# One PSUM tile per bank, with halved evacuations and another order at the start of each FFN and of the convolution

## The chip, the core and the metric

The kernel runs on one core of one Trainium2 chip. TensorE (PE) multiplies, VectorE (DVE) and ScalarE (ACT) do the elementwise work, GpSimd (POOL) does little here, and SyncE (SP) issues the weight loads. The metric is the time of one execution in device microseconds (us); the median of a few runs is compared. PSUM, into which TensorE writes, has eight banks of 128 partitions by 512 float32.

## What is computed

An encoder of four layers on 256 tokens of width 1024. Each layer is a half-step SwiGLU FFN, one token mixer, and a second half-step FFN; the four mixers are dilated attention, a convolution module, a Fourier mixer and a chunked gated linear attention (GLA). Each sub-layer starts with an RMS norm, and a last one ends the trunk.

```python
def _swiglu(h, w1, w3, w2):
    return (jax.nn.silu(h @ w1) * (h @ w3)) @ w2          # 1024 -> 2816 -> 1024

def reference(x, norm_g, ...):
    h = x
    for i in range(DEPTH):                                # 4 layers, mixer m = i % 4
        h = h + 0.5 * _swiglu(_rmsnorm(h, norm_g[i, 0]), ffn_w1[i, 0], ffn_w3[i, 0], ffn_w2[i, 0])
        u = _rmsnorm(h, norm_g[i, 1])
        ...                                               # mix = attention, convolution, Fourier or GLA of u
        h = h + mix
        h = h + 0.5 * _swiglu(_rmsnorm(h, norm_g[i, 2]), ffn_w1[i, 1], ffn_w3[i, 1], ffn_w2[i, 1])
    return _rmsnorm(h, final_norm_g)

def _conv_module(u, w_pw1, b_pw1, w_dw, b_dw, ln_g, ln_b, w_pw2, b_pw2):
    a, gate = jnp.split(u @ w_pw1 + b_pw1, 2, axis=-1)
    z = a * jax.nn.sigmoid(gate)
    ...                                                   # depthwise convolution of width 31, LayerNorm, silu, w_pw2
```

## The kernel before

**Numbers.** Every float32 operand of a matmul is a pair: a rounded high part and the rest as a low part, and a product is three matmuls (high by high, high by low, low by high). In the FFN, `wide` packs two of the three into one matmul of 512 columns, so that a result stands in two halves q=0 and q=1 of a bank, which are added when it is read.

**Weights.** All weights come as blocks of 128 by 2048 float32 (1 MB), in one fixed order. SP loads a block into one of four `raw` buffers (L158); `split_block` makes the pair `w` (four buffers): ACT copies the high part (L167), and DVE subtracts it from `raw` for the low part (L170). After the matmuls of a block `done()` counts a free buffer in `pend`; `pump(n)` issues up to n of the splits that are pending at that place in the code, with `between` ahead of the DVE half. The instructions of each engine run in the order in which the code issues them, and the framework sets semaphores between engines from the tiles that instructions read and write.

**PSUM.** The eight banks are four tiles `P00` to `P11` of [128, 1024], each two banks; `bank(half, j)` is a half of such a tile and `two(half, n)` a whole one. In the rows both are called P. `ab()` gives out the four banks of one half in turn, `dbank(j)` those of the other.

**FFN** (`ffn`). The 2816 hidden columns go in NG = 11 groups of 256: each takes a block of w1 into PA and one of w3 into PB, 32 matmuls per block (16 of 256 columns and 16 of 512), and every second group is followed by a block of w2 (`half_add`) into the other four banks. What follows a group is: `parts`, an ACT copy of q=1 out of PSUM (L461); `add`, the DVE addition of q=0 (L465); `times_r`, the norm's factor (L468); silu (L471); `gate` (L474) and the split of its result `g` (L622 on ACT, L623 on DVE). `half_close` adds the finished banks to the residual h (L277). The factor R of the norm comes from `stats` and three Newton `steps` on DVE.

**Mixers.** Projections go into `ab()` banks and are evacuated singly: in attention `qk` (L1017), the scores' `s` (L1046) and `og`; in the convolution `ar` (L694) and `gr` (L699) of the gated linear unit, then `zp` (L704); in the Fourier mixer `m` (L623); in GLA `ks` (L1237, L1244) and per head and chunk `t` (L1391). Each mixer ends with a down projection that is added to h (L277, L280).

**What sets the order.** There is no planner. TensorE's program order is the code's; between it and the two elementwise engines only the semaphores decide.

Of the kernel before, what the change touches and what calls it, by code (L numbers as in the profile page):

```python
# [18 lines left out]
NG = DFF // 256  # L19
# [19 lines left out]
class Enc:  # L39
    def __init__(self, ctx, tc, a, stages):  # L40
        self.ctx, self.tc, self.nc, self.a = ctx, tc, tc.nc, a
        self.stages = stages
        P = lambda name, bufs=1, **kw: ctx.enter_context(tc.tile_pool(name=name, bufs=bufs, **kw))
        self.const = P("const")
        self.wp = P("wp")
        self.hp = P("hp")
        self.ev = None
        self.ps = P("ps", space=PSUM)
        self.dram = P("dram", space=bass.MemoryType.DRAM)
        self.nm = 0  # L50
        self.banks = [[self.ps.tile([128, 1024], F32, name=f"P{i}{n}") for n in range(2)] for i in range(2)]
        self.lower, self.nab, self.held = 0, 3, []


# [16 lines left out]
        return self.bank(1 - self.lower, j)  # L71

    def bank(self, half, j):
        return self.banks[half][j // 2][:, 512 * (j % 2):512 * (j % 2) + 512]

    def two(self, half, n):

        return self.banks[half][n].rearrange("p (c q n) -> p c q n", c=2, q=2)

    def mm(self, out, lhsT, rhs, start, stop):  # L80
        return self.nc.tensor.matmul(out, lhsT, rhs, start=start, stop=stop, skip_group_check=True)  # L81
# [177 lines left out]
    def close_pair(self, j, P, scale, bias=None):  # L259

        nc = self.nc
        h = self.h[j]
        P = P if isinstance(P, list) else [self.v2(P)]
        if self.unperm:
            assert bias is None
            hn = self.sb(self.ev, [128, 2, 256], F32, "sl", 2)
            for p in P[1:]:
                nc.vector.scalar_tensor_tensor(h, p, float(scale), h, ALU.mult, ALU.add)
            for c in range(2):
                nc.vector.scalar_tensor_tensor(hn[:, c].rearrange("p (m a) -> p a m", a=4),  # L270
                                               P[0][:, c].rearrange("p (a m) -> p a m", a=4), float(scale),
                                               h[:, c].rearrange("p (a m) -> p a m", a=4), ALU.mult, ALU.add)
            nc.gpsimd.tensor_copy(h, hn)
            h = hn
        elif bias is None:
            for p in P:
                nc.vector.scalar_tensor_tensor(h, p, float(scale), h, ALU.mult, ALU.add)  # L277
        else:
            for c in range(2):
                nc.vector.scalar_tensor_tensor(h[:, c], P[0][:, c], bias[c], h[:, c], ALU.add, ALU.add)  # L280
        self.flush_acc()
        if j < 3 or not (self.short() or self.row_norm()):
            self.normed(j, h)
            self.square(j, h)
        else:
            self.square(j, h)
            self.normed(j, h)
# [145 lines left out]
    def wide(self, p, c, w, k, x, start, stop):  # L433


        self.mm(p[:, c, 0], w[:, 1, k], x[:, 0], start, False)
        self.mm(p[:, c], w[:, 0, k], x, False, stop)

    def ffn(self, l, s):
        nc = self.nc  # L440
# [6 lines left out]
        PA, PB = (self.two(up_half, n) for n in range(2))  # L447
# [6 lines left out]
        def take_up(n, i, P):  # L454
            up(self.take((n, i)), P)
            self.done()

        def parts(P, tag):

            t = self.sb(self.ev, [128, 2, 256], F32, tag, 2)  # L460
            nc.scalar.activation(t, P[:, :, 1], AF.Copy)  # L461
            return t

        def add(t, P):
            nc.vector.tensor_tensor(t, t, P[:, :, 0], ALU.add)  # L465

        def times_r(t):
            nc.vector.tensor_tensor(t, t, self.Rb(), ALU.mult)  # L468

        def silu(t):  # L470
            nc.scalar.activation(t, t, AF.Silu)  # L471

        def gate(i, sl, br):
            nc.vector.tensor_tensor(br, sl, br, ALU.mult)  # L474
            g[i] = self.pair(self.ev, [128, 2, 256], "g", NG)
            self.split(br, g[i])
# [5 lines left out]
        for n, ks in enumerate(cuts):  # L482
# [20 lines left out]
        br0 = parts(PB, "br")  # L503
        steps.pop(0)()
        add(br0, PB)
        self.pump(held)
        steps.pop(0)()
        for i in range(1, NG):
            take_up("w1", i, PA)
            sl = parts(PA, "sl")  # L510
            if i == 1:
                add(sl, PA)
                times_r(sl0)
                silu(sl0)
                self.pump(1, between=lambda: times_r(sl))
                silu(sl)
                times_r(sl0)
                gate(0, sl0, br0)
                self.pump(1)
            else:  # L520
                self.pump(1, between=lambda: (add(sl, PA), times_r(sl)))
                silu(sl)
            if i == 4 and pre:
                self.pre = pre()
            take_up("w3", i, PB)
            br = parts(PB, "br")
            self.pump(1, between=lambda: (times_r(sl), add(br, PB)))
            gate(i, sl, br)
            if i % 2 == 0:
                p = i // 2 - 1  # L530
                if i == NG - 1:
                    break
                self.half_add(self.take(("w2", 0, p)), [g[2 * p], g[2 * p + 1]], 0, p == 0)
                self.done()
                self.pump(1)

        p = NP - 1
        self.half_add(self.take(("w2", 0, p)), [g[2 * p], g[2 * p + 1]], 0)
# [2 lines left out]
        w = self.take(("w2",))  # L541
# [8 lines left out]
        for p in range(NP):  # L550
# [3 lines left out]
            w = self.take(("w2", 1, p))  # L554
# [27 lines left out]

    def half_close(self, half, j):
        P = self.two(1 - self.lower, j)
        self.close_pair(2 * half + j, [P[:, :, 1], P[:, :, 0]], 0.5)


    D4 = None
# [73 lines left out]
    def mix1(self):  # L662
        nc = self.nc
# [11 lines left out]
        def pw1(i, names=("pa", "pg"), hook={}):  # L675
            ws = [self.take((n, i)) for n in names]
            ps = [self.ab() for _ in names]
            for k in range(8):
                for w, p in zip(ws, ps):
                    for c in range(2):  # L680
                        sl = slice(128 * c, 128 * c + 128)
                        self.mm3(p[:, 256 * c:256 * c + 256], w[:, :, k, sl], self.xk(k),
                                 start=k == 0 and c == 0, stop=k == 7)
                if k in hook:
                    hook[k]()
            self.done(len(names))
            return ps
# [4 lines left out]
        def glu_a(i, A):  # L692
            ar = self.sb(ev, [128, 2, 256], F32, "ar")
            nc.vector.tensor_tensor(ar, self.v2(A), self.Rb(), ALU.mult)  # L694
            return ar

        def glu_g(i, ar, G):
            gr = self.sb(ev, [128, 2, 256], F32, "gr")
            nc.vector.tensor_tensor(gr, self.v2(G), self.Rb(), ALU.mult)  # L699
            for c in range(2):  # L700
                nc.scalar.activation(gr[:, c], gr[:, c], AF.Sigmoid, bias=self.col(("bp1", 8 + 2 * i + c)))
            zp = zps[(1, 0, 2, 1)[i]]
            for c in range(2):
                nc.vector.scalar_tensor_tensor(zp[:, c, PAD:PAD + S], ar[:, c], self.col(("bp1", 2 * i + c)), gr[:, c],  # L704
                                               ALU.add, ALU.mult)
# [55 lines left out]
        def factor():  # L761
            steps = self.stats(True)
            self.pump(1)
            for f in steps:
                f()
            self.pump(1)

        A0, G0 = pw1(0, hook={4: factor})
        self.pump()
        A1, = pw1(1, ("pa",))  # L770
        glu_g(0, glu_a(0, A0), G0)
        ar = glu_a(1, A1)
        taps = lambda n: lambda: taps_v(n)
        self.pump()
        G1, = pw1(1, ("pg",))
        copies(0, (0,))
        glu_g(1, ar, G1)
        self.pump(between=taps(2))
        A2, = pw1(2, ("pa",))
        copies(0, (1,))  # L780
        ar = glu_a(2, A2)
        self.pump(between=taps(4))
        G2, = pw1(2, ("pg",))
        dw(0)
# [34 lines left out]
        var, r, q = (self.sb(ev, [128, 2], F32, n) for n in ("lv", "lr", "lq"))  # L819
# [18 lines left out]
        half = [slice(128 * t, 128 * t + 128) for t in range(2)]  # L838
# [34 lines left out]
        w = self.take(("wp2", 0))  # L873
# [9 lines left out]
        w = [self.take(("wp2", j)) for j in (2, 3)]  # L883
# [739 lines left out]
```

## Time and profile before

| | |
|---|---|
| median of three runs | 2093.06 us (2091.75 to 2093.56) |
| profiled execution | 2094.18 us |
| its span, first to last instruction | 2092.4 us |
| TensorE busy | 1949.4 us (93%) |
| VectorE busy | 1390.8 us (66%) |
| ScalarE busy | 978.3 us (47%) |
| DMA, mean of 16 engines | 45% |
| mean granted TensorE clock | 0.972 |

The profiled execution lies 1.8 us above its span. The stages follow one another in the span as FFN 0 to 205 us, attention to 378, two FFNs to 764, convolution to 901, two FFNs to 1279, Fourier to 1333, two FFNs to 1711, GLA to 1891, and the last FFN with the final norm.

### The profile page before, as it was taken

How to read it: one execution, taken by the hardware profiler on the slowest of the kernel's cores; microseconds unless marked ns; L12 is line 12 of the kernel's file. 1: busy time of each engine (PE TensorE's matmuls, PEld its weight loads, DVE VectorE, ACT ScalarE, POOL GpSimd, SP SyncE). 2: the span in 40 equal slices, each digit the busy share in tenths (PEclk: the TensorE clock that was granted, in tenths of full speed). 3: DMA queues.
4: the chain of work that ended last, by engine and by line, in shares of the span. 5: the costliest groups of instructions: out<-in, count | busy, mean ns of one | idle time of the engine just before them, and what ended most of it. 6: DMA issues, size and time to landing. Idle time of an engine off the chain costs nothing.

```text
span 2092.4 us, 28814 instructions
## 1 busy us (share of the span) xinstructions
PE 1949.4 (93%) x12272; PEld 1712.3 (82%) x12272; DVE 1390.8 (66%) x1614; ACT 978.3 (47%) x1097; POOL 34.5 (2%) x55
## 2 busy tenths in 40 slices
PE   7999978899989998799999999999999997889998
PEld 6888977788878887588888888888888886778887
DVE  7766455776686775777667675676677664557764
ACT  6444433544444543444445444454445445444443
POOL 0000000000040000000000000000000000000000
PEclk9999989999999999899999999999999998999999
DMA  6554521355445543135545553355545552223551
GB/s 244 201 191 173 210 97 65 141 202 183 179 165 185 197 158 126 51 132 201 192 170 185 198 181 141 113 210 182 204 166 195 196 182 81 101 101 125 198 182 60
DMA packets 48642, 338.08 MB, mean 162 GB/s; under 512 B 5568, under 2 KB 5744, under 8 KB 8192
## 3 DMA queue, kind: packets, MB, share of 16 engines
q1 hardware_dynamic: 47952, 335.11, 44.7%
q8 instruction: 96, 1.57, 0.3%
q0 software_dynamic: 560, 1.12, 0.2%
q14 instruction: 34, 0.28, 0.0%
HBM read 335.16 MB, written 1.05 MB: 161 GB/s over the span
## 4 chain that ended last, share of the span: by engine, by line
PE 79%; DVE 11%; ACT 6%; issue 3%; DMA 0%; SPq 0%; ACTq 0%; DVEq 0%
PE P L81 79%; DVE w L170 4%; ACT w L167 3%; DVE sl L468 1%; DVE zc L748 1%; DVE s L1046 1%; DVE br L474 1%; PE P L84 0%; DVE m L1049 0%; DMA h<-in_x_dram 0%; DVE h L277 0%; DVE sl L465 0%; DVE br L465 0%; ACT sl L471 0%; DVE g L623 0%
## 5 line engine op out<-in xcount | busy, mean ns | idle before, releaser
L81 PE MATMUL P<-x,w 128*128 128x256 f32 x6976 | 1183.4, 330 | 80.8 <-DVE qk L1017 17.7
L81 PEld LDWEIGHTS P<-x,w 128*128 128x128 f32 x6976 | 1040.2, 192 | 219.8 <-DVE qk L1017 18.5
L170 DVE TENSOR_TENSOR w<-raw,w 128x2048 fp32r<-128x2048 f32 x315 | 719.7, 2293 | 273.1 <-ACT w L167 272.9
L167 ACT ACTIVATE w<-raw 128x2048 fp32r<-128x2048 f32 x315 | 597.6, 1906 | 65.2 <-PE P L81 44.8
L81 PE MATMUL P<-g,w 128*128 128x256 f32 (+1 forms) x2816 | 504.2, 337 | 7.1 <-ACT g L622 4.3
L81 PEld LDWEIGHTS P<-g,w 128*128 128x128 f32 x2816 | 433.3, 187 | 73.7 <-ACT g L622 6.9
L622 ACT ACTIVATE g<-br 128x512 fp32r<-128x512 f32 x88 | 55.6, 632 | 279.1 <-DVE br L474 279.1
L461 ACT ACTIVATE br<-P 128x512 f32<-128x512 f32 x88 | 52.4, 596 | 171.2 <-PE P L81 171.1
L468 DVE TENSOR_TENSOR sl<-sl,R 128x512 f32<-128x512 f32 x176 | 121.7, 695 | 2.5
L461 ACT ACTIVATE sl<-P 128x512 f32<-128x512 f32 x88 | 52.0, 591 | 142.9 <-PE P L81 139.8
L81 PE MATMUL P<-w,x 128*128 128x256 f32 (+1 forms) x720 | 95.7, 294 | 8.4 <-ACT Em L1334 3.4
L623 DVE TENSOR_TENSOR g<-br,g 128x512 fp32r<-128x512 f32 x88 | 61.2, 695 | 61.5 <-ACT g L622 61.5
L81 PEld LDWEIGHTS P<-w,x 128*128 128x128 f32 x720 | 92.7, 202 | 10.3 <-ACT Em L1334 3.8
L298 ACT ACTIVATE x<-h,cols 128x256 fp32r<-128x256 f32 x88 | 39.9, 500 | 115.2 <-DVE h L277 91.8
L465 DVE TENSOR_TENSOR sl<-sl,P 128x512 f32<-128x512 f32 x88 | 60.2, 684 | 47.0 <-ACT sl L461 46.7
L465 DVE TENSOR_TENSOR br<-br,P 128x512 f32<-128x512 f32 x88 | 60.3, 686 | 43.7 <-ACT br L461 43.7
L277 DVE SCALAR_TENSOR_TENSOR h<-P,h 128x512 f32<-128x512 f32 x64 | 44.1, 690 | 47.2 <-PE P L81 46.2
L471 ACT ACTIVATE sl<-sl 128x512 f32<-128x512 f32 x88 | 54.7, 622 | 13.2 <-DVE sl L468 13.1
L474 DVE TENSOR_TENSOR br<-sl,br 128x512 f32<-128x512 f32 x88 | 60.6, 689 | 0.3
L300 DVE SCALAR_TENSOR_TENSOR x<-h,cols,x 128x256 fp32r<-128x256 f32 x88 | 38.9, 483 | 16.9 <-ACT x L298 16.7
L1017 DVE TENSOR_TENSOR qk<-P,Rqk 128x512 f32<-128x512 f32 x12 | 8.3, 688 | 32.6 <-PE P L81 32.6
L81 PE MATMUL P<-og,w 128*128 128x256 f32 x192 | 25.3, 286 | 3.2 <-DVE h L277 3.2
(229 smaller groups left out, 796.3 us busy)
## 6 DMA issues: line engine op xcount, KB each, us to landing
raw<-in_ffn_w_dram SPq DMA_DIRECT2D x262, 1024.0 KB, 4.8
raw<-in_attn_w_qk_dram SPq DMA_DIRECT2D x12, 1024.0 KB, 4.8
raw<-in_conv_w_pw_dram SPq DMA_DIRECT2D x12, 1024.0 KB, 5.0
raw<-in_gla_w_in_dram SPq DMA_DIRECT2D x12, 1024.0 KB, 5.2
raw<-in_attn_w_v_dram SPq DMA_DIRECT2D x6, 1024.0 KB, 5.1
raw<-in_fnet_w_dram SPq DMA_DIRECT2D x4, 1024.0 KB, 6.3
raw<-in_gla_w_o_dram SPq DMA_DIRECT2D x4, 1024.0 KB, 4.8
raw<-in_ffn_w_dram SPq DMA_DIRECT2D x8, 256.0 KB, 6.7
```

What stands on the lines that cost most here:

```text
L81: return self.nc.tensor.matmul(out, lhsT, rhs, start=start, stop=stop, skip_group_check=True)
L167: self.nc.scalar.activation(w[:, 0], raw, AF.Copy)
L170: (eng or self.nc.vector).tensor_tensor(w[:, 1], raw, f32(w[:, 0]), ALU.subtract)
L277: nc.vector.scalar_tensor_tensor(h, p, float(scale), h, ALU.mult, ALU.add)
L298: nc.scalar.activation(xh[:, c], h[:, c], AF.Copy, scale=g[c])
L461: nc.scalar.activation(t, P[:, :, 1], AF.Copy)
L465: nc.vector.tensor_tensor(t, t, P[:, :, 0], ALU.add)
L468: nc.vector.tensor_tensor(t, t, self.Rb(), ALU.mult)
L471: nc.scalar.activation(t, t, AF.Silu)
L474: nc.vector.tensor_tensor(br, sl, br, ALU.mult)
L622: self.nc.scalar.activation(p[:, 0], src, AF.Copy)
L623: self.nc.vector.tensor_tensor(p[:, 1], src, f32(p[:, 0]), ALU.subtract)
```

## The change

Each of the eight banks becomes a tile of its own, A0 to A3 and B0 to B3; `two()` returns a list of two views, one per bank. What read or wrote both banks of a pair in one instruction does it bank by bank: the FFN's copies and additions are two of 128x256 where there was one of 128x512, and `half_close` has four additions where there were two. In the FFN the code of the first groups is issued in another order, the last group's gate stands ahead of its split, and the `pump(1)` behind `half_add` becomes `pump()`. In the convolution the first products are evacuated inside a split (`between`), and two pumps are placed differently.

```diff
-        self.banks = [[self.ps.tile([128, 1024], F32, name=f"P{i}{n}") for n in range(2)] for i in range(2)]
+        self.banks = [[self.ps.tile([128, 512], F32, name=f"{'AB'[i]}{n}") for n in range(4)] for i in range(2)]
...
-        return self.banks[half][j // 2][:, 512 * (j % 2):512 * (j % 2) + 512]
+        return self.banks[half][j]
...
-        return self.banks[half][n].rearrange("p (c q n) -> p c q n", c=2, q=2)
+        return [self.v2(self.bank(half, 2 * n + c)) for c in range(2)]
...
-            nc.scalar.activation(t, P[:, :, 1], AF.Copy)
+            for c in range(2):
+                nc.scalar.activation(t[:, c], P[c][:, 1], AF.Copy)
...
-            nc.vector.tensor_tensor(t, t, P[:, :, 0], ALU.add)
+            for c in range(2):
+                nc.vector.tensor_tensor(t[:, c], t[:, c], P[c][:, 0], ALU.add)
...
         self.pump(held)
         steps.pop(0)()
+        self.pump(1)
         for i in range(1, NG):
             take_up("w1", i, PA)
             sl = parts(PA, "sl")
             if i == 1:
-                add(sl, PA)
-                times_r(sl0)
+                self.pump(1, between=lambda: (add(sl, PA), times_r(sl0), times_r(sl)))
                 silu(sl0)
-                self.pump(1, between=lambda: times_r(sl))
-                silu(sl)
-                times_r(sl0)
-                gate(0, sl0, br0)
-                self.pump(1)
             else:
                 self.pump(1, between=lambda: (add(sl, PA), times_r(sl)))
-                silu(sl)
+            silu(sl)
...
-            self.pump(1, between=lambda: (times_r(sl), add(br, PB)))
-            gate(i, sl, br)
+            if i == 1:
+                add(br, PB)
+                times_r(sl0)
+                gate(0, sl0, br0)
+                self.pump(1, between=lambda: times_r(sl))
+                gate(i, sl, br)
+            elif i < NG - 1:
+                self.pump(1, between=lambda: (times_r(sl), add(br, PB)))
+                gate(i, sl, br)
+            else:
+                times_r(sl)
+                add(br, PB)
+                gate(i, sl, br)
+                self.pump(1)
...
                 self.half_add(self.take(("w2", 0, p)), [g[2 * p], g[2 * p + 1]], 0, p == 0)
                 self.done()
-                self.pump(1)
+                self.pump()
...
             steps = self.stats(True)
             self.pump(1)
             for f in steps:
                 f()
-            self.pump(1)
 
         A0, G0 = pw1(0, hook={4: factor})
-        self.pump()
         A1, = pw1(1, ("pa",))
-        glu_g(0, glu_a(0, A0), G0)
+        r0 = []
+        self.pump(1, between=lambda: r0.extend((glu_a(0, A0), glu_r(G0))))
+        glu_g(0, r0[0], G0, r0[1])
```

DVE's program at the start of the FFN at 1090 us, from the third Newton step on; w is a split's low part, sl and br the two evacuations, g the gated result, P_69 and P_70 the tiles PA and PB. Before:

```order
L465 TENSOR_TENSOR sl_8830<-sl_8830,P_69 128x512
L468 TENSOR_TENSOR sl_8762<-sl_8762,R_8746 128x512
L468 TENSOR_TENSOR sl_8830<-sl_8830,R_8746 128x512
L170 TENSOR_TENSOR w_8835<-raw_8599,w_8835 128x2048
L468 TENSOR_TENSOR sl_8762<-sl_8762,R_8746 128x512
L474 TENSOR_TENSOR br_8784<-sl_8762,br_8784 128x512
L623 TENSOR_TENSOR g_8844<-br_8784,g_8844 128x512
L170 TENSOR_TENSOR w_8847<-raw_8636,w_8847 128x2048
L468 TENSOR_TENSOR sl_8830<-sl_8830,R_8746 128x512
L465 TENSOR_TENSOR br_8884<-br_8884,P_70 128x512
```

The same place of the changed kernel, where A_69 to A_72 are the four banks:

```order
L170 TENSOR_TENSOR w_9010<-raw_8771,w_9010 128x2048
L471 TENSOR_TENSOR sl_9047<-sl_9047,A_69 128x256
L471 TENSOR_TENSOR sl_9047<-sl_9047,A_70 128x256
L474 TENSOR_TENSOR sl_8975<-sl_8975,R_8959 128x512
L474 TENSOR_TENSOR sl_9047<-sl_9047,R_8959 128x512
L170 TENSOR_TENSOR w_9050<-raw_8808,w_9050 128x2048
L471 TENSOR_TENSOR br_9093<-br_9093,A_71 128x256
L471 TENSOR_TENSOR br_9093<-br_9093,A_72 128x256
L474 TENSOR_TENSOR sl_8975<-sl_8975,R_8959 128x512
L480 TENSOR_TENSOR br_8999<-sl_8975,br_8999 128x512
L636 TENSOR_TENSOR g_9100<-br_8999,g_9100 128x512
```

One split (w_9010) now stands ahead of the second group's evacuation, and the evacuation of br ahead of the first gate instead of behind the gate and a further split.

DVE's program in the convolution, from the last Newton step to the second `gr`; P_71 and P_72 are two-bank tiles. Before:

```order
L369 SCALAR_TENSOR_TENSOR R_6128<-nRu_6133,R_6128 128x256
L170 TENSOR_TENSOR w_6150<-raw_5919,w_6150 128x2048
L170 TENSOR_TENSOR w_6191<-raw_5956,w_6191 128x2048
L170 TENSOR_TENSOR w_6196<-raw_5993,w_6196 128x2048
L694 TENSOR_TENSOR ar_6249<-P_72,R_6128 128x512
L699 TENSOR_TENSOR gr_6251<-P_72,R_6128 128x512
L704 SCALAR_TENSOR_TENSOR zp_531_6058<-ar_6249,cols,gr_6251 128x256 x2
L694 TENSOR_TENSOR ar_6257<-P_71,R_6128 128x512
L170 TENSOR_TENSOR w_6259<-raw_6139,w_6259 128x2048
L699 TENSOR_TENSOR gr_6333<-P_71,R_6128 128x512
```

The same place of the changed kernel, with one bank per tile:

```order
L373 SCALAR_TENSOR_TENSOR R_6289<-nRu_6294,R_6289 128x256
L707 TENSOR_TENSOR ar_6397<-B_75,R_6289 128x512
L712 TENSOR_TENSOR gr_6399<-B_76,R_6289 128x512
L170 TENSOR_TENSOR w_6395<-raw_6076,w_6395 128x2048
L721 SCALAR_TENSOR_TENSOR zp_533_6219<-ar_6397,cols,gr_6399 128x256 x2
L707 TENSOR_TENSOR ar_6408<-B_73,R_6289 128x512
L170 TENSOR_TENSOR w_6410<-raw_6113,w_6410 128x2048
L170 TENSOR_TENSOR w_6415<-raw_6150,w_6415 128x2048
L712 TENSOR_TENSOR gr_6489<-B_74,R_6289 128x512
```

The three splits ahead of the first `ar` are now one behind `gr` and two behind the second `ar`; the second `ar` and `gr`, which read the two halves of P_71, read the tiles B_73 and B_74.

## Rows read from the trace of the kernel before

**Rows 1.** The page's first part (busy time, share of the span, instructions) and the chain that ended last, by line.
```profile
span 2092.4 us, 28814 instructions
PE 1949.4 (93%) x12272; PEld 1712.3 (82%) x12272; DVE 1390.8 (66%) x1614; ACT 978.3 (47%) x1097; POOL 34.5 (2%) x55
PE P L81 79%; DVE w L170 4%; ACT w L167 3%; DVE sl L468 1%; DVE zc L748 1%; DVE s L1046 1%; DVE br L474 1%; PE P L84 0%; DVE m L1049 0%; DMA h<-in_x_dram 0%; DVE h L277 0%; DVE sl L465 0%; DVE br L465 0%; ACT sl L471 0%; DVE g L623 0%
```

**Rows 2.** Busy time of each engine in stretches of the span, then the mean granted clock, the DMA share and GB/s: attention, the FFN at 568, the convolution, the FFN at 901, Fourier, GLA, and the sum over all twelve stages.
```profile
205.00:378.43 173.43, 145.58 (x1189) 139.00 (x1188) 93.00 (x152) 68.57 (x95) 0.00 (x0) 0.94 0.34 125
...
568.26:763.93 195.67, 188.93 (x1060) 163.43 (x1058) 140.53 (x135) 91.25 (x91) 24.24 (x29) 0.98 0.51 179
763.93:901.04 137.11, 111.77 (x1185) 95.76 (x1184) 89.72 (x159) 56.46 (x92) 0.42 (x6) 0.88 0.26 93
901.04:1089.94 188.90, 185.44 (x1060) 161.02 (x1059) 133.48 (x132) 90.78 (x90) 0.00 (x0) 1.00 0.51 184
...
1278.87:1333.12 54.25, 46.62 (x350) 45.71 (x348) 27.40 (x42) 21.10 (x32) 0.00 (x0) 0.91 0.27 98
...
1710.70:1890.50 179.80, 146.23 (x1022) 130.76 (x1021) 91.66 (x175) 84.13 (x126) 0.55 (x2) 0.90 0.26 94
...
sum 2093.00, PE 1949.43 PEld 1712.28 DVE 1390.81 ACT 978.29 POOL 34.48; mean PE 162.45 PEld 142.69 DVE 115.90 ACT 81.52 POOL 2.87
```

**Rows 3.** What TensorE waited for, by engine and line: us in total, times, the longest.
```profile
PE P L81 <- DVE qk L1017: 17.7, 4, 5.7
PE P L81 <- DVE w L170: 12.3, 10, 1.8
PE P L81 <- DVE br L465: 12.2, 8, 2.1
PE P L81 <- DVE h L277: 9.6, 4, 5.6
PE P L81 <- DVE ar L694: 9.3, 2, 8.9
PE P L81 <- DVE h L280: 8.7, 4, 4.4
...
PE P L81 <- DVE t L1391: 7.3, 2, 3.7
PE P L81 <- DVE ks L1244: 5.9, 1, 5.9
```

**Rows 4.** The timeline of attention around one step (start, us, engine, line, tiles, count, idle time before and what ended it), and the stretch from 275.3 as a row of the view of Rows 2.
```profile
275.28 2.29 DVE L170 TENSOR_TENSOR w<-raw,w 128x2048 fp32r<-128x2048 f32 x1 [1.11 <-ACT w L167]
277.49 0.68 DVE L1017 TENSOR_TENSOR qk<-P,Rqk 128x512 f32<-128x512 f32 x1
...
278.22 2.93 PE L81 MATMUL P<-x,w 128*128 128x256 f32 x12 [5.60 <-DVE qk L1017]
...
275.30:282.10 6.80, 3.88 (x18) 3.88 (x19) 2.87 (x2) 0.06 (x1) 0.00 (x0) 0.50 0.46 154
```

**Rows 5.** The timeline of the convolution from the end of the Newton steps.
```profile
778.82 6.69 DVE L170 TENSOR_TENSOR w<-raw,w 128x2048 fp32r<-128x2048 f32 x3
...
789.68 0.69 DVE L694 TENSOR_TENSOR ar<-P,R 128x512 f32<-128x512 f32 x1
...
790.51 7.56 PE L81 MATMUL P<-x,w 128*128 128x256 f32 x48 [8.93 <-DVE ar L694]
```

**Rows 6.** The timeline at the start of the FFN at 1090 us.
```profile
1111.63 2.29 DVE L170 TENSOR_TENSOR w<-raw,w 128x2048 fp32r<-128x2048 f32 x1 [1.90 <-ACT w L167]
...
1113.97 5.92 PE L81 MATMUL P<-x,w 128*128 128x256 f32 x32 [1.16 <-DVE w L170]
...
1117.75 2.29 DVE L170 TENSOR_TENSOR w<-raw,w 128x2048 fp32r<-128x2048 f32 x1 [1.11 <-ACT w L167]
...
1120.56 0.68 DVE L465 TENSOR_TENSOR br<-br,P 128x512 f32<-128x512 f32 x1
...
1121.30 4.98 PE L81 MATMUL P<-x,w 128*128 128x256 f32 x27 [1.41 <-DVE br L465]
```

**Rows 7.** The timeline behind the last group of the FFN at 568 us.
```profile
726.00 2.29 DVE L170 TENSOR_TENSOR w<-raw,w 128x2048 fp32r<-128x2048 f32 x1 [1.12 <-ACT w L167]
728.21 0.68 DVE L474 TENSOR_TENSOR br<-sl,br 128x512 f32<-128x512 f32 x1
...
729.61 0.38 PE L81 MATMUL P<-g,w 128*128 128x256 f32 x1 [0.54 <-ACT g L622]
730.34 2.95 PE L81 MATMUL P<-g,w 128*128 128x512 f32 x15 [0.34 <-DVE g L623]
```

**Rows 8.** Five groups of instructions by line and shape (busy us, mean ns of one, idle time before): ACT's half of a weight split, the FFN's ACT copy and DVE addition out of PSUM, and two evacuations of 128x256.
```profile
L167 ACT ACTIVATE w<-raw 128x2048 fp32r<-128x2048 f32 x315 | 597.6, 1906 | 65.2 <-PE P L81 44.8 <-issue 20.1 <-ACT w L167 0.3
...
L461 ACT ACTIVATE sl<-P 128x512 f32<-128x512 f32 x88 | 52.0, 591 | 142.9 <-PE P L81 139.8 <-issue 3.2
...
L465 DVE TENSOR_TENSOR sl<-sl,P 128x512 f32<-128x512 f32 x88 | 60.2, 684 | 47.0 <-ACT sl L461 46.7
...
L406 DVE TENSOR_SCALAR R<-P 128x256 f32<-128x256 f32 x9 | 3.8, 420 | 2.4 <-PE P L81 2.4
...
L1334 ACT ACTIVATE Em<-P 128x256 f32<-128x256 f32 x8 | 3.1, 388 | 0.0
```

**Rows 9.** The timeline of TensorE alone in the middle of an FFN: four groups of 32 matmuls in one row.
```profile
617.77 22.35 PE L81 MATMUL P<-x,w 128*128 128x256 f32 x128
```

More of the change, by code (lines that the diff above doesn't have):

```diff
@@ L266, in close_pair @@
             hn = self.sb(self.ev, [128, 2, 256], F32, "sl", 2)
-            for p in P[1:]:
-                nc.vector.scalar_tensor_tensor(h, p, float(scale), h, ALU.mult, ALU.add)
+            for c in range(2):
+                nc.vector.scalar_tensor_tensor(h[:, c], P[1][c], float(scale), h[:, c], ALU.mult, ALU.add)
             for c in range(2):
                 nc.vector.scalar_tensor_tensor(hn[:, c].rearrange("p (m a) -> p a m", a=4),
-                                               P[0][:, c].rearrange("p (a m) -> p a m", a=4), float(scale),
+                                               P[0][c].rearrange("p (a m) -> p a m", a=4), float(scale),
                                                h[:, c].rearrange("p (a m) -> p a m", a=4), ALU.mult, ALU.add)
@@ L276, in close_pair @@
             for p in P:
-                nc.vector.scalar_tensor_tensor(h, p, float(scale), h, ALU.mult, ALU.add)
+                if isinstance(p, list):
+                    for c in range(2):
+                        nc.vector.scalar_tensor_tensor(h[:, c], p[c], float(scale), h[:, c], ALU.mult, ALU.add)
+                else:
+                    nc.vector.scalar_tensor_tensor(h, p, float(scale), h, ALU.mult, ALU.add)
         else:
@@ L433, in wide @@
     def wide(self, p, c, w, k, x, start, stop):
-        self.mm(p[:, c, 0], w[:, 1, k], x[:, 0], start, False)
-        self.mm(p[:, c], w[:, 0, k], x, False, stop)
+        self.mm(p[c][:, 0], w[:, 1, k], x[:, 0], start, False)
+        self.mm(p[c], w[:, 0, k], x, False, stop)
     def ffn(self, l, s):
@@ L460, in parts @@
             t = self.sb(self.ev, [128, 2, 256], F32, tag, 2)
-            nc.scalar.activation(t, P[:, :, 1], AF.Copy)
+            for c in range(2):
+                nc.scalar.activation(t[:, c], P[c][:, 1], AF.Copy)
             return t
         def add(t, P):
-            nc.vector.tensor_tensor(t, t, P[:, :, 0], ALU.add)
+            for c in range(2):
+                nc.vector.tensor_tensor(t[:, c], t[:, c], P[c][:, 0], ALU.add)
         def times_r(t):
@@ L526, in ffn @@
             br = parts(PB, "br")
-            self.pump(1, between=lambda: (times_r(sl), add(br, PB)))
-            gate(i, sl, br)
+            if i == 1:
[7 more added lines that the diff above has]
+                gate(i, sl, br)
+            else:
+                times_r(sl)
+                add(br, PB)
+                gate(i, sl, br)
+                self.pump(1)
             if i % 2 == 0:
@@ L584, in half_close @@
         P = self.two(1 - self.lower, j)
-        self.close_pair(2 * half + j, [P[:, :, 1], P[:, :, 0]], 0.5)
+        self.close_pair(2 * half + j, [[p[:, q] for p in P] for q in (1, 0)], 0.5)
     D4 = None
@@ L695, in glu_a, with glu_r, glu_g @@
             return ar
-        def glu_g(i, ar, G):
+        def glu_r(G):
             gr = self.sb(ev, [128, 2, 256], F32, "gr")
             nc.vector.tensor_tensor(gr, self.v2(G), self.Rb(), ALU.mult)
+            return gr
+        def glu_g(i, ar, G, gr=None):
+            gr = gr or glu_r(G)
             for c in range(2):
```

## Prediction

> **What bounds the kernel now.** I read the page's first part and its chain, then the stretches by stage, then what TensorE waits for, and last the timeline at the longest of these waits. TensorE is busy for 1949.4 of 2092.4 us, and 79% of the chain that ended last is its matmuls; VectorE (66%) and ScalarE (47%) have room on the average [rows 1]. The change takes away no matmul. So what it can win is TensorE's idle time, 2093.0 − 1949.4 = 143.6 us over all stages, and the time lost where the clock stood at the lower of its two levels (1.2 in place of 2.4 GHz).
>
> By stage the two kinds of stage differ [rows 2]. The FFN at 901 us is idle for 188.90 − 185.44 = 3.5 us and has a clock of 1.00. The mixers are idle for 27.9 (attention), 25.3 (convolution), 7.6 (Fourier) and 33.6 us (GLA), 94.4 together, with clocks of 0.94, 0.88, 0.91 and 0.90. A clock of 0.94 over 173.43 us loses at most 0.06 × 173.43 = 10.4 us of full-speed work; for the four that is 10.4 + 16.5 + 4.9 + 18.0 = 49.8. TensorE is idle in part of these stretches: the one at 275.3 us has a clock of 0.50 for 6.80 us, but only 3.88 of them are busy, which at full clock would take 1.9 [rows 4]. I therefore count some 60 to 70% of the 49.8, about 32.
>
> The list of waits names who ends the idle time: `qk` 17.7 us in 4 waits, a weight split 12.3 in 10, `br` 12.2 in 8, h 9.6 and 8.7, `ar` 9.3, `t` 7.3, `ks` 5.9 [rows 3]. Together 83.0 of the 143.6, and all VectorE instructions, though VectorE is far from full. The timelines say why.
>
> **The wait for a neighbour.** In attention, the matmuls that start at 278.22 wait 5.60 us for `qk`, which ended just before [rows 4]. They are the next projection, they need neither `qk` nor its bank. They write the other bank of the two-bank tile that `qk` reads, and the semaphores are set by tile. `qk` itself ran late because it stood behind a split of 2.29 us on VectorE, for which it has no need. In the convolution it is worse: three splits (6.69 us), then the first gated unit, then the second `ar` at 789.68, and the matmuls at 790.51, which want only the bank beside that `ar`, wait 8.93 us [rows 5]. The waits for `ks`, for `t` and most of those for h read the same way, by the code: a projection, a triangle sum or the next FFN's first group goes into a bank whose twin is still being read. With a tile per bank these are no waits at all. The code order of the changed program leaves TensorE's own sequence as it is; it takes away what it waits for.
>
> **What the mixers give.** Each number is a stage's idle time and clock loss less what I believe are true waits.
> Attention: three waits of 5.6 for `qk` (16.9 of the 17.7), some 3 us behind scores and `og`, 2.6 in the first projections, 3.2 at the end, and about 7 of clock, since the three stretches at half clock each follow one of the long waits: 33.
> Convolution: 25.3 idle. The LayerNorm in its middle is a true chain over several engines (column sums, square root, broadcast) and keeps its gaps and most of its low clock. What goes is the 8.93 [rows 5], 1.9 behind `zp`, about 1.4 in short ones, 5 of the waits for h behind the down projection, and a little clock: 18.5.
> Fourier: one wait of 3.3 behind two splits, 3.3 for h, 1.1 in short ones and some 3 of clock: 10.5.
> GLA: 33.6 idle and about 13 of clock. `ks` 5.9, two for `t` (7.3), h 5.6 and some twelve of 0.5 to 2 us are of the same kind; I leave about 6 for true chains: 41.
> Together 103 of the 94.4 + 32 = 126 that the four mixers lose. No row shows a mixer without the neighbour's wait. The bounds are 0 (each true wait stands right behind the false one) and 126; I take 103 because in the two timelines that I show the late instruction is held by splits of weights, not by data that the matmul needs.
>
> **The FFNs.** Their waits are true ones, and the reordering moves them. At the start of the FFN at 1090, TensorE waits 1.16 us for a split that runs at 1111.63, and 1.41 us for `br`, whose addition at 1120.56 stands behind a split of 2.29 at 1117.75 [rows 6]. TensorE came at 1113.97 − 1.16 = 1112.8 and at 1121.30 − 1.41 = 1119.9. In the changed order one more split precedes the second group, so that this block is done one VectorE turn (a split and its neighbours, by my estimate some 6 us) earlier, near 1107.4; and `br` is added ahead of the gate and the split, near 1114.5. Both are before the time of need, even when TensorE itself comes 1.2 us earlier. What gets later is the first gate, but its g is first read two groups later, 11 us. Each such start gives 2.57; six FFNs read alike: 15.4. The first FFN and that at 568 us hold the rest of the two rows, 12.3 + 12.2 − 15.4 = 9.1 [rows 3]; I take 8.6, with the second's low clock (0.98) in it.
> Behind the last group TensorE waits 0.54 + 0.34 us for the two halves of g, because the gate at 728.21 stands behind a split of 2.29 at 726.00 [rows 7]. With the gate first it starts 2.2 us earlier, more than 0.88: all of it goes, in eight FFNs 7.0. FFNs together: 31.
>
> **What it costs.** Two instructions replace one at 176 ScalarE copies and as many VectorE additions. A VectorE evacuation of 128x256 takes 0.420 us and one of 128x512 0.684: +0.156 a pair. ScalarE: 2 × 0.388 − 0.591 = +0.185 [rows 8]. That is 27 us more work on VectorE and 33 on ScalarE, off the path: a group of 32 matmuls takes 22.35 / 4 = 5.59 us [rows 9], the copy and addition that free PA take 0.59 + 0.68 and now 0.34 more, and PA is written again only after PB's whole group. Were that cover gone, it would cost up to 176 × 0.34 = 60 us. The four closing additions instead of two weigh 32 × 4 × 0.42 − 64 × 0.69 = 10 us more at the longest, over 32 places, and start as early as before. `pump()` behind the second-half product lets two splits go in a row; its price is the last rival's. SP's loads follow the splits and keep their order. I put all these at 0, and keep 60 as the other end.
> This is where a rule speaks against the change. The Trainium skill, page "Perfetto Trace Analysis", section "Optimizing Scalar/DVE Operations", gives every instruction a fixed access overhead (on PSUM about 125 ns on VectorE and 51 ns on ScalarE, in the profile about twice that) and advises larger operations where the engine is saturated. By its figures a pair costs an estimated 0.25 and 0.10, 62 us over 176; the trace agrees in size with its 60 [rows 8]. The same section recommends smaller pieces where these engines are not saturated but stall others.
>
> **The sum.** 2094.2 − 103 − 31 = 1960 us for a profiled execution; the median of the runs shown lies 1.1 us lower, which is within what I can tell. A difference under 0.2% (4 us) is about what a measurement of this kernel can't tell from none.
>
> **The rivals.**
> *True waits take over in the mixers* (15%): behind each wait for a neighbour stands one for data; with TensorE early, VectorE's queue of scores, splits and Newton steps is the bound. For it: VectorE is at 93.0 of 173.43 us in attention and 89.72 of 137.11 in the convolution, in bursts. Against: its work there is no longer than half to two thirds of the stage. Half of the 103 goes: 2012 us.
> *The halves come onto the path* (4%): if VectorE's turn of a group is full in the FFN, the 60 us are paid: 2021. Against it: 133.48 busy of 188.90 [rows 2].
> *More than I count goes* (5%): GLA and convolution lose nearly all of their idle time and the clock stays high: 126 + 31, about 1937.
> *The neighbours' waits stay* (2%), because the same semaphore is also needed for another reason: only the FFNs gain, 2063. Another 1% lies within 4 us of before.
> *Slower* (3%): the second split of `pump()` behind each half product. ScalarE's copy of 1.91 [rows 8] stands ahead of the next group's evacuation, and waits until a buffer comes free at the end of the product. TensorE's next group lasts 5.59, so it stalls only when the copy is over 5.59 − 1.91 = 3.7 us late. There are 4 to 5 such places in each of eight FFNs, about 40. To eat 134 us each must cost 3.4 us beyond that slack, the copy being 7 us late. No row shows such lateness: the splits in mid-FFN don't hold TensorE over four groups in a row [rows 9].
>
> **How the numbers follow.** The forecast as told has 70%, and alone runs from 1945 to 1982. With the first rival's middle and the fifth's lower end, 1936 to 2015 leaves out about 17%: the halves, the two small ones, slower, and the upper half of the first rival in part. Faster by over 0.2%: 70 + 15 + 4 + 5 + 2 = 96%; within: 1%; slower: 3%.
>
> **What would show it.** TensorE's busy time near 1925 (less of it at half clock) and its idle time near 35; no wait for `qk` or `ar` over 1 us; granted clock near 1.00 in attention, still under 0.95 in the convolution; FFN stretches of about 185.5 us; no wait for a split or `br` at their starts; copies and additions of 128x256 twice 88 each. Wrong it would be if `qk` or `t` still end waits of several us, if waits for h in the next FFN's start merely move, or if the FFN stretches grow.

## Result and profile after

The changed kernel takes 1935.65 us (median of four runs, 1933.23 to 1938.04) against 2093.31 for the kernel before; the ratio is 0.9247 with an interval of 0.9231 to 0.9263. The forecast was 1960 and its range ended at 1936, so the direction and the mechanism held and the size did not: 158 us were won where 134 were expected. The median lies 0.35 us below the range, less than its own runs differ by, but 24 us below the forecast itself.

The page's first part, the granted clock in 40 slices and the chain by line of the changed kernel, which answer to [rows 1]:

```profile
span 1935.0 us, 29203 instructions
...
PE 1906.1 (99%) x12272; PEld 1683.3 (87%) x12272; DVE 1397.5 (72%) x1850; ACT 995.4 (51%) x1273; POOL 35.0 (2%) x55
...
PEclk9999999999999999899999999999999999999999
...
PE B L81 50%; PE A L81 41%; DVE w L170 1%; ACT w L167 1%; DVE zc L765 1%; DMA raw<-in_ffn_w_dram 0%; PE A L84 0%; DMA h<-in_x_dram 0%; ACT zc L880 0%; PE B L84 0%; DVE h L279 0%; DVE acc L355 0%; DVE x L304 0%; DVE sl L474 0%; ACT x L302 0%
```

The number of TensorE instructions is the same, and their busy time fell by 43 us. Its matmuls in L81 now are 91% of the chain that ended last, with A and B for the eight bank tiles.

The stretches of the changed kernel, in the order of [rows 2]: attention, the FFN after it but one, the convolution, the FFN behind that, Fourier, GLA. Columns as there: the stretch, its length, busy PE, PEld, DVE, ACT, POOL, then the mean granted clock, the DMA share and GB/s.

```profile
200.79:337.53 136.74, 136.43 (x1189) 131.96 (x1187) 88.36 (x145) 64.43 (x89) 0.00 (x0) 1.00 0.41 151
524.84:712.04 187.20, 185.58 (x1060) 161.07 (x1059) 141.72 (x164) 93.29 (x113) 25.46 (x29) 1.00 0.53 187
712.04:824.24 112.20, 105.80 (x1186) 91.38 (x1184) 88.02 (x162) 55.35 (x93) 0.42 (x6) 0.95 0.31 113
824.24:1008.75 184.51, 184.51 (x1060) 161.02 (x1059) 135.88 (x160) 94.49 (x112) 0.00 (x0) 1.00 0.54 189
1193.32:1234.84 41.52, 41.52 (x349) 41.31 (x348) 26.15 (x46) 20.11 (x33) 0.00 (x0) 1.00 0.35 126
1603.93:1736.81 132.88, 132.87 (x1021) 121.37 (x1020) 86.91 (x174) 80.82 (x124) 0.55 (x2) 0.97 0.35 124
```

Attention went from 173.4 to 136.7 us, the convolution from 137.1 to 112.2, Fourier from 54.3 to 41.5 and GLA from 179.8 to 132.9. Apart from the convolution, these four mixers have next to no idle time left (0.31 us in attention, 0.00 in Fourier and 0.01 in GLA).

What TensorE waits for now, the whole list but for three entries of under 1 us, answering to [rows 3]:

```profile
PE A L81 <- DVE w L636: 7.3, 1, 7.3
PE A L81 <- ACT zs L635: 2.4, 1, 2.4
PE A L84 <- DVE h L279: 1.9, 1, 1.9
PE B L81 <- DVE lr L395: 1.5, 1, 1.5
PE B L81 <- DVE R L341: 1.4, 1, 1.4
PE A L81 <- DVE sl L471: 1.3, 1, 1.3
PE B L81 <- DVE sl L471: 1.2, 2, 1.0
PE A L81 <- ACT x L879: 1.1, 1, 1.1
PE A L81 <- DVE w L170: 1.1, 1, 1.1
PE B L81 <- DVE zc L833: 1.1, 1, 1.1
```

No `qk`, `ar`, `ks`, `t` and no `br` is on it. The first entry is the start of the program, where TensorE waits for its first weights (7.6 us before); `zs`, `lr`, `zc` and x are the LayerNorm of the convolution, the true chain of the forecast.

### The profile page after: what moved, and what is told of

Same layout as the page of the kernel before. It is cut to its first block, busy times and chain, and to the rows that moved or that the text cites. A ratio compares the mean times of both kernels' runs of the same rounds, so it can differ in the third digit from the quotient of the medians.

```text
span 1935.0 us, 29203 instructions
## 1 busy us (share of the span) xinstructions
PE 1906.1 (99%) x12272; PEld 1683.3 (87%) x12272; DVE 1397.5 (72%) x1850; ACT 995.4 (51%) x1273; POOL 35.0 (2%) x55
## 4 chain that ended last, share of the span: by engine, by line
PE 92%; DVE 5%; ACT 2%; DMA 1%; issue 1%; SPq 0%; DVEq 0%; ACTq 0%
PE B L81 50%; PE A L81 41%; DVE w L170 1%; ACT w L167 1%; DVE zc L765 1%; DMA raw<-in_ffn_w_dram 0%; PE A L84 0%; DMA h<-in_x_dram 0%; ACT zc L880 0%; PE B L84 0%; DVE h L279 0%; DVE acc L355 0%; DVE x L304 0%; DVE sl L474 0%; ACT x L302 0%
## 5 line engine op out<-in xcount | busy, mean ns | idle before, releaser
L81 PE MATMUL B<-x,w 128*128 128x256 f32 (+1 forms) x3968 | 643.5, 322 | 1.4 <-DVE sl L471 1.2
L81 PEld LDWEIGHTS B<-x,w 128*128 128x128 f32 x3968 | 571.5, 190 | 71.1 <-issue 5.5
L81 PE MATMUL A<-x,w 128*128 128x256 f32 x3008 | 522.4, 335 | 10.9 <-DVE w L636 7.3
L81 PEld LDWEIGHTS A<-x,w 128*128 128x128 f32 x3008 | 455.5, 189 | 74.9 <-DVE w L636 7.3
L81 PE MATMUL B<-g,w 128*128 128x256 f32 (+1 forms) x1408 | 251.1, 336 | 0.3 <-DVE w L170 0.2
L81 PE MATMUL A<-g,w 128*128 128x256 f32 (+1 forms) x1408 | 250.3, 336 | 0.0
L81 PEld LDWEIGHTS B<-g,w 128*128 128x128 f32 x1408 | 216.5, 187 | 32.2 <-DVE g L636 0.5
L81 PEld LDWEIGHTS A<-g,w 128*128 128x128 f32 x1408 | 216.6, 187 | 31.4
L81 PE MATMUL B<-w,x 128*128 128x256 f32 (+1 forms) x504 | 62.6, 284 | 0.0
L81 PEld LDWEIGHTS B<-w,x 128*128 128x128 f32 x504 | 61.3, 191 | 0.4 <-issue 0.3
```

## Experiments

### What the tiles do alone, and what the order does alone

Against the kernel before, the tiles alone are:

```diff
-        self.banks = [[self.ps.tile([128, 1024], F32, name=f"P{i}{n}") for n in range(2)] for i in range(2)]
+        self.banks = [[self.ps.tile([128, 512], F32, name=f"{'AB'[i]}{n}") for n in range(4)] for i in range(2)]
...
-            nc.scalar.activation(t, P[:, :, 1], AF.Copy)
+            for c in range(2):
+                nc.scalar.activation(t[:, c], P[c][:, 1], AF.Copy)
```

and the order alone, which has the rest of the change:

```diff
+        self.pump(1)
         for i in range(1, NG):
...
-                self.pump(1)
+                self.pump()
...
-        glu_g(0, glu_a(0, A0), G0)
+        r0 = []
+        self.pump(1, between=lambda: r0.extend((glu_a(0, A0), glu_r(G0))))
+        glu_g(0, r0[0], G0, r0[1])
```

> Eight tiles of one bank, with the halved instructions, but the order of before in FFN and convolution. Theory (every wait that the mixers lost was one for the neighbouring bank; the FFNs gained only by their order): the mixers' stages become 36.6 + 24.9 + 12.7 + 46.9 = 121 us shorter as in the changed kernel, or up to 9 less if the convolution needs its own order too, and the FFNs stay: 1972 to 1981 us. Rival (the new order, which runs one split further ahead, gave the mixers a good part): over 2000 us.

> The new order in FFN and convolution on the four two-bank tiles of before, no halved instruction. Theory: only the FFNs' 36 us and at most 9 in the convolution, 2048 to 2057 us; the waits for qk, t and ks stay as long as before. Rival (order matters for the mixers): below 2030 us, with waits for qk under 4 us.

Measured: tiles alone 1970.4 us (ratio 0.9412, 0.9394 to 0.9429); order alone 2046.7 us (0.9774, 0.9759 to 0.9789). Both are far from the rivals and near the theory, each about 1.5 us below its nearer end. The stretches of attention, Fourier and GLA with the tiles alone:

```profile
204.11:340.84 136.73, 136.42 (x1188) 131.94 (x1187) 89.96 (x145) 64.69 (x89) 0.00 (x0) 1.00 0.43 158
1218.72:1259.93 41.21, 41.21 (x350) 41.21 (x349) 26.74 (x43) 20.63 (x31) 0.00 (x0) 1.00 0.36 128
1635.98:1765.83 129.85, 129.84 (x1021) 119.17 (x1020) 87.50 (x171) 81.36 (x122) 0.56 (x2) 1.00 0.36 128
```

and what TensorE waits for in the kernel with the order alone:

```profile
PE P L81 <- DVE qk L1028: 17.7, 4, 5.7
PE P L81 <- DVE h L277: 9.6, 4, 5.6
PE P L81 <- DVE h L280: 8.7, 4, 4.5
PE P L81 <- DVE t L1402: 7.3, 2, 3.7
...
PE P L81 <- DVE ks L1255: 5.9, 1, 5.9
...
PE P L81 <- DVE ar L701: 3.0, 2, 2.6
...
PE P L81 <- DVE m L630: 1.4, 1, 1.4
...
PE P L81 <- DVE w L170: 1.0, 2, 0.7
```

These three mixers are as short with the tiles alone as in the changed kernel, to 0.3 us (GLA to 3.0, of which the section on the clock tells). With the order alone the waits for `qk`, h, `t` and `ks` stand to the tenth of a us as in [rows 3], while those for a split fall from 12.3 to 1.0, those for `br` are gone, and `ar` falls from 9.3 to 3.0. So tiles and order act on different stages, but for two. The convolution is 137.1 us before, 115.7 with the tiles, 129.5 with the order and 112.2 with both. Fourier is 54.3 before and 50.3 with the order alone, where its wait for `m` falls from 3.3 to 1.4 and the lower clock holds for less of it; on top of the tiles the order gives nothing there (41.2 and 41.5). The wait of before, and the stretch of Fourier with the order alone:

```profile
PE P L81 <- DVE m L623: 3.3, 1, 3.3
```

```profile
1245.04:1295.37 50.33, 44.21 (x349) 43.09 (x348) 26.59 (x44) 20.44 (x33) 0.00 (x0) 0.97 0.28 105
```

The eight FFNs together take 1547.9 us before, 1543.7 with the tiles, 1511.6 with the order and 1511.7 with both.

### The changed kernel with the FFN's old order

> The changed kernel with the FFN's order of before; tiles and the convolution's order as changed. Theory: the FFNs lose their 36 us again and nothing else moves, 1972 us; the difference to the kernel with tiles alone is what the convolution's order gives on top of the tiles, 0 to 9 us. Rival (the FFN's order, by running ahead, serves the mixers too): over 1985 us.

Measured: 1968.2 us (0.9394, 0.9376 to 0.9412). It lies 4 us under the 1972 of the theory and far from the rival's 1985: the FFN's order serves the FFNs. The convolution's stretch is 113.1 us, 2.6 less than with the tiles alone; on the two-bank tiles the same order gave 7.6. The medians of the two kernels (1968.2 and 1970.4) are too close to tell them apart. In the eight profiles that have both the one-bank tiles and the convolution's new order its stretch runs from 110.6 to 113.1 us, partly by the clock, so that the order gives some 3 to 5 us when the neighbours' waits are gone, with only one profile without it to compare.

### The price of the halves, and of quarters

Halves on the two-bank tiles of before, and then quarters in the changed kernel, the additions likewise:

```diff
-            nc.scalar.activation(t, P[:, :, 1], AF.Copy)
+            for c in range(2):
+                nc.scalar.activation(t[:, c], P[:, c, 1], AF.Copy)
```

```diff
             for c in range(2):
-                nc.scalar.activation(t[:, c], P[c][:, 1], AF.Copy)
+                for s in (slice(0, 128), slice(128, 256)):
+                    nc.scalar.activation(t[:, c, s], P[c][:, 1, s], AF.Copy)
```

> The kernel before with the 176 FFN copies and 176 additions each cut into two of 128x256, on the same two-bank tiles. Theory: 27 us more VectorE and 33 us more ScalarE work are hidden, 2093 us within 4. Rival (the halves are on the path): up to 60 us slower, 2153 us.

> The changed kernel with each FFN copy and addition cut once more, into four of 128x128: the fixed price of the cut is paid twice more (352 more instructions on each of VectorE and ScalarE). Theory: hidden in the middle of every FFN, but the evacuations of the first groups, which stand on VectorE with the Newton steps and the splits, get later: 1 to 2 us in each of eight FFNs at most, 1936 to 1950 us. Rival (every evacuation counts): some 60 us and more, over 1990 us.

Measured: halves alone 2094.9 us (1.0007, 0.9997 to 1.0016), no difference that the times can tell; quarters 1935.9 us (0.9254, 0.9238 to 0.9270), the changed kernel's time within its interval. The groups of VectorE's additions and ScalarE's copies of one bank's tile by line and shape (busy us, mean ns of one, idle time before), first in the changed kernel and then with quarters:

```profile
L471 DVE TENSOR_TENSOR sl<-sl,A 128x256 f32<-128x256 f32 x88 | 33.0, 416 | 14.4 <-ACT sl L466 14.4
...
L466 ACT ACTIVATE sl<-A 128x256 f32<-128x256 f32 x88 | 29.8, 377 | 53.1 <-PE A L81 53.1
```

```profile
L473 DVE TENSOR_TENSOR sl<-sl,A 128x128 f32<-128x128 f32 x176 | 38.4, 279 | 13.7 <-ACT sl L467 13.7
...
L467 ACT ACTIVATE sl<-A 128x128 f32<-128x128 f32 x176 | 34.1, 275 | 51.0 <-PE A L81 51.0
```

A half took 0.416 and 0.377 us, which the nearest rows of before had at 0.420 and 0.388 [rows 8]; a quarter takes 0.279 and 0.275. The records of neighbours overlap, so the price is better read from the busy time: an addition of 512 elements keeps VectorE busy for 4 × 38.4 / 176 = 0.87 us in quarters, 2 × 33.0 / 88 = 0.75 in halves, and 60.2 / 88 = 0.68 in one piece [rows 8]. Little of it reaches the end. In the profiles the eight FFNs are 2.4 us longer with the halves alone (1550.3 in place of 1547.9) and 2.1 longer with the quarters (1513.8 in place of 1511.7), which the times can't tell from nothing. The Trainium skill, page "Perfetto Trace Analysis", section "Optimizing Scalar/DVE Operations", ties its advice for larger operations to a saturated engine; the trace agrees with that condition, at 72% and 51% busy.

### What a wait costs

The changed kernel with the last group's gate behind the split again:

```diff
-            elif i < NG - 1:
-                self.pump(1, between=lambda: (times_r(sl), add(br, PB)))
-                gate(i, sl, br)
             else:
-                times_r(sl)
-                add(br, PB)
+                self.pump(1, between=lambda: (times_r(sl), add(br, PB)))
                 gate(i, sl, br)
-                self.pump(1)
```

> The changed kernel with the last group's gate behind the split again, as before; all else as changed. It puts two waits back in each of eight FFNs. Theory (a wait costs TensorE more than its idle row: from one matmul's start to the next, before against after, the two cost 1.42 us and not the 0.54 + 0.34 of the row): 8 x 1.4 = 11 us over the changed kernel's 1935.6, about 1947; some more if the halved addition makes the gate later. Rival (the idle rows are the whole cost): 8 x 0.88 = 7 us, about 1943.

Measured: 1941.0 us (0.9281, 0.9266 to 0.9295), 5.3 over the changed kernel and under both expectations. The timeline behind the last group of the FFN at 1238 us says why:

```profile
1388.24 0.69 DVE L480 TENSOR_TENSOR br<-sl,br 128x512 f32<-128x512 f32 x1
...
1389.65 0.38 PE L81 MATMUL A<-g,w 128*128 128x256 f32 x1 [0.28 <-ACT g L630]
1390.37 2.95 PE L81 MATMUL A<-g,w 128*128 128x512 f32 x15 [0.34 <-DVE g L631]
```

The waits are 0.28 + 0.34 = 0.62 us, not 0.88, since TensorE comes a little later there; the expectation had taken their size over from [rows 7]. But the stretch of this FFN is 185.66 us against 184.52 in the changed kernel, 1.14 longer for 0.62 us of idle time. Matmul by matmul (start to next start, the two traces laid over each other) the excess is 0.43 us at the first wait, 0.61 at the second and 0.10 at the matmul after, and nothing elsewhere. All eight FFNs have the same three steps at this place. So two waits with an idle time of 0.62 cost 1.14, about 0.26 us each beyond their row. The profile's busy time thus holds a part of what a wait costs; a tenth of a us of it is a slower matmul behind the wait, the rest stands ahead of it, where matmuls' ends are modelled. The median of the whole kernel does not show it as it stands: 8 × 1.14 = 9.1 would be 1944.8, and 1941.0 came. In the two profiles the sum comes out otherwise: the eight places cost 9.1, but a wait of 1.4 us for R in the first FFN is absent, and the wait for h in the last norm is 1.1 shorter because TensorE comes later to it, so that with smaller differences the FFNs together are 7.3 us longer. The convolution and GLA are 4.6 us shorter, as the lower clock holds for less time in them (the clock is the subject below), and the span is 2.8 longer.

### Running a split ahead

```diff
                 self.done()
-                self.pump()
+                self.pump(1)
```

> The changed kernel with pump(1) in place of pump() behind the half product, so that a split more is pending when an FFN starts. Theory: the split that the second group of an FFN needs is late again, 1.2 to 2.9 us in each of six or seven FFNs, 1943 to 1955 us, with waits for a split (w) at their starts. Rival (running ahead has no part in the starts, the extra pump(1) alone does it): 1936 us within 3.

Measured: 1934.3 us (0.9246, 0.9230 to 0.9263), the changed kernel's time. My theory falls and the rival stands. The waits for a split are these:

```profile
PE A L81 <- DVE w L170: 3.3, 2, 2.1
...
PE B L81 <- DVE w L170: 0.7, 1, 0.7
```

That is three places where the changed kernel has 1.1 + 0.2 us in two, and the four FFNs between the convolution and GLA take 184.3 to 184.6 us, against 184.5 to 184.6 there. The extra `pump(1)` behind the third Newton step does the work by itself. The last rival of the prediction, a second split that stalls ScalarE behind the half product, has no footing either: with and without the second split the two kernels can't be told apart (1935.7 and 1934.3 us).

### A version with later transposes, and the clock in GLA

The one wait of over 1.5 us outside the first FFN and the convolution was that for h ahead of the last norm's first transpose.

```diff
-            if p < 2 and self.nstage >= len(self.stages):
-                self.fin_transpose(p)
+            if 0 < p < 3 and self.nstage >= len(self.stages):
+                self.fin_transpose(p - 1)
```

> The changed kernel with the first two transposes of the last norm issued one block of w2 later, behind matmuls that need nothing from the closing. Theory: the wait of 1.92 us for h ahead of the first transpose goes with its hidden part, 2.2 us, 1933.4 us, and the last FFN's stretch becomes 196.0 instead of 198.2. Rival (the next thing, the second transpose or the last norm, waits as long): 1935.6 us.

Measured: 1932.2 us (0.9235, 0.9221 to 0.9249). The last FFN's stretch is 195.86 us in place of 198.23, 2.4 less for an idle row of 1.92, and its list of waits has no such entry any more. The intervals of this and the changed kernel overlap, so the stretch decides it: it is 195.9 to 196.2 us in the three profiles with the later transposes and 196.9 to 198.5 in the changed kernel and the three experiments that change something else in the FFN.

In the changed kernel GLA took 132.9 us and with the tiles alone 129.9, both without idle time. The difference is the clock, as two stretches of the changed kernel show, the second right behind the first:

```profile
1623.26:1628.40 5.14, 5.14 (x20) 2.60 (x20) 3.83 (x3) 4.19 (x7) 0.00 (x0) 1.00 0.61 207
1628.40:1635.20 6.80, 6.80 (x24) 5.07 (x25) 0.06 (x1) 4.50 (x7) 0.00 (x0) 0.50 0.38 152
```

TensorE is busy throughout both, and the clock goes from the higher level to the lower all the same. Around the fall stand GLA's four gate products, whose contraction has 17 rows, between projections: three of them end ahead of it. I tried to move the fall by their place.

On top of the later transposes, the four products were spread (first) or put together (second):

```diff
-        p2 = qkproj(2, {4 + i: lambda dt=dt: gate_a(*dt) for i, dt in enumerate(dts)})
+        p2 = qkproj(2, {(2, 4, 6, 7)[i]: lambda dt=dt: gate_a(*dt) for i, dt in enumerate(dts)})
```

```diff
-        p2 = qkproj(2, {4 + i: lambda dt=dt: gate_a(*dt) for i, dt in enumerate(dts)})
+        p2 = qkproj(2, {5: lambda: [gate_a(*dt) for dt in dts]})
```

> The kernel with the later transposes, and in GLA the four 17-row gate products behind steps 2, 4, 6 and 7 of the third projection in place of 4, 5, 6 and 7. In four of seven profiles with one-bank tiles the clock stood at 0.50 for 3.4 to 10.2 us just behind these products, with no idle time of TensorE ahead of it. Theory (the run of 17-row products close together is what lets the clock fall): spread out, no fall, the GLA stretch 129.9 us, about 1930 us. Rival (the fall has another cause, or comes by chance): falls as before in some runs, 1932 us; or a wait where the first product stands ahead of its factor R.

> The same with all four 17-row gate products behind step 5, one after the other. Theory: the clock falls behind them in the profile and in most runs, 3 to 5 us over the kernel with spread products, 1933 to 1936 us. Rival (their closeness has no part): no difference to the spread ones within 2 us.

Measured: spread 1930.7 us (0.9225, 0.9212 to 0.9238), together 1931.4 us (0.9228, 0.9215 to 0.9241). The profile with the products together has a fall of 3.4 us at this place and 1.2 us of waits, a GLA stretch of 130.8; the spread one has none and 129.95. That is the direction of the theory, but the times are 0.7 us apart where 3 to 5 were expected. The stretch of GLA with the products spread:

```profile
1601.38:1731.33 129.95, 129.94 (x1022) 119.29 (x1021) 86.88 (x174) 80.75 (x124) 0.55 (x2) 1.00 0.35 126
```

One profile without a fall says little, since three of the seven with the products in their old place have none either. By the times the rival holds, and what makes the clock fall here stays open.

The kernel with the spread products, which has the later transposes too, has the lowest median of all: its four runs (1929.6 to 1932.0) lie below the four of the changed kernel (1933.2 to 1938.0), but not below those with the later transposes alone (1929.7 to 1934.1).

## Why the prediction missed

By stage, with the length of the stretch in the two profiles (the eight FFNs summed):

| stage | idle + clock loss before, as forecast | forecast gain | measured gain | of it idle time, clock, rest |
|---|---|---|---|---|
| attention | 27.9 + 7 | 33 | 36.6 | 27.5, 7.7, 1.4 |
| convolution | 25.3 + a little | 18.5 | 24.9 | 19.0, 5.6, 0.3 |
| Fourier | 7.6 + 3 | 10.5 | 12.7 | 7.6, 4.8, 0.3 |
| GLA | 33.6 + 13 | 41 | 46.9 | 33.6, 10.3, 3.0 |
| FFNs | | 31 | 36.2 | 26.4, 4.4, 5.4 |
| sum | | 134 | 157.4 | 114, 32.8, 10.5 |

**The mechanism was right.** The mixers' waits were waits for the neighbouring bank, and a tile per bank ended them; the FFNs gained by their order; the halves cost next to nothing (about 2 us by the profiles). Each of these has its own experiment.

**The step that failed is "less what I believe are true waits".** From the idle time and the clock loss of each mixer I took off a part for true chains: 6 us of idle time in GLA, and some 2 in attention, where the waits that I counted come to 25.7 of 27.9. No such chain shows there: with the tiles alone the two stages keep 0.01 and 0.31 us of idle time. In Fourier nothing was held back. In the convolution there is a true chain, the LayerNorm, but it is shorter. I let 17.2 us of idle time go and 19.0 went, and its low clock, most of which I kept, gave 5.6. I had not followed these waits to what they needed, but held back a margin, and then added it up as if it were a finding. Together that is 9.5 us of idle time and about 4 of clock, over half of the 23 that were missing.

**A second term had no row.** Idle time fell from 143.0 to 28.9, by 114 us (the 143.6 of the forecast is taken over a stretch that ends 0.6 us behind the span). The clock gave an estimated 32.8: busy time at the lower level fell from 81.0 to 15.4 us in the clock records of the two traces, and half of the difference is counted as lost time. These make 146.9, and the stages gained 157.4. The other 10.5 lie inside what the profile calls busy. Laid over the changed kernel matmul by matmul, 64 of the waits of before, all those that the change took away outside the stretches at the lower clock, had 65.7 us of idle time and cost 14.6 beyond it, 0.23 each; matmuls without a wait, 2.5 us slower in all, and the estimate for the clock account for the other 4. The sum went by idle rows alone, and so did the bound of "126 + 31, about 1937", where the range ended: the mixers' 121 stayed below their 126, and the FFNs' 36.2 went past their 31, by about their part without a row. The FFN at 901 us shows it best: 3.46 us of idle time in four waits, and 188.90 − 184.51 = 4.39 us of gain. The forecast for it was 185.5.

**Clock.** I counted some 24 of the 32.8 by stage, although I had put the four mixers at about 32 myself. What I left out is most of the convolution's (19.9 us of busy time at the lower level became 8.6), a third of Fourier's, and much of that of the FFN at 568 us; GLA's 13 were 10.3. The clock is at 1.00 in attention, as said, and at 0.954 in the convolution, where I had said under 0.95; GLA's 0.97 has no idle time behind it.

**Other steps.** The copy and addition of a half were sized from the nearest rows to 3%, but the 27 and 33 us of work made of them were too much, since records overlap: with the halves alone VectorE is busy for 11.2 us more and ScalarE for 10.8, so the 60 us of the rival rest on a price that is too high. The FFN's start came as forecast, by one more split ahead of the second group; the `pump()` behind the half product has no part in it. That `ar` waits would go by the tiles was right, and the convolution's new order, for which the forecast had no term of its own, then has some 3 to 5 us left to give. Of the chances, 5% for the case that came (nearly all idle time gone, the clock high) was too little: the rows for `qk`, `ar`, `t` and `ks` all pointed to one kind of wait, and no row to a second one behind it.

## What to carry to other kernels

When a tile covers two PSUM banks, a write into one bank waits for the readers of the other; here one-bank tiles alone took away 123 of 2093 us. A wait of TensorE for a VectorE instruction whose result its next matmul does not use is the sign of it, and one tile per bank costs only instructions that elementwise engines with room can hide (here all but about 2 us). A wait costs TensorE more than its idle row (here 0.23 us more on the average of 64 waits), and a long one its clock as well (at the wait of 5.60 us in [rows 4] the lower level held for 6.8 us); price it from one matmul start to the next, and take a discount for unseen chains only where a dependency has been named.

## What the runs showed of the hardware

The clock fell to its lower level for 3.4 to 10.2 us at one place of GLA in five of the nine profiles with one-bank tiles (the changed kernel and eight experiments), in four of them with no gap of TensorE ahead of it; 10.2 us at the lower level cost 4.6 (a GLA stretch of 134.5 us in place of 129.9). I had expected it to fall only behind idle time. The changed kernel's four runs follow their mean granted clock: 1938.0 us at 0.992, 1937.2 at 0.994, 1934.1 at 0.995 and 1933.2 at 0.996.
